# The down products of a group of MLP units placed one up block later, behind the next group's first block, in a two-layer decoder trunk on one core

## Chip, cores and metric

The kernel runs on one core of one Trainium2 chip. The metric is device time in microseconds (us) from the first to the last instruction's end, as the runs report it; lower is better.

## The reference

One inference step of a two-layer decoder trunk, in float32, over 1,024 prompt tokens and 32 new tokens (1,056 columns). Layer 0 is a gated linear recurrence, layer 1 dilated window attention; each ends in an MLP of 4,096 hidden units on a width of 1,024:

```python
def _sqrelu_mlp(x, w_up, w_down):
    return jnp.square(jax.nn.relu(x @ w_up)) @ w_down
...
        x = x + h.astype(x.dtype)
        x = x + _sqrelu_mlp(_rmsnorm(x, mlp_norm[layer]), mlp_w_up[layer], mlp_w_down[layer]).astype(x.dtype)
```

The change lies in the two MLPs alone.

## The kernel before

**Exact pairs.** Each operand of a product is kept as a pair, a rounded high part and the low rest. A product of 128 by 128 weights with a chunk of tokens is three matmuls: high by high, high by low, low by high (L182 to L184 for the up blocks, L772 to L774 for the down products). The tokens lie in three chunks of 384, 384 and 288 columns (c = 0, 1, 2).

**Groups.** `mlp` goes over the 32 blocks of hidden units in eight groups (`NG`) of four. For each group it makes the four up blocks, j = 0 to 3, and after them the down products of the group, which add into the residual `xr`. An up block is 72 matmuls: for each chunk eight steps of K by three. Its results leave PSUM chunk by chunk in `ev_up`: ScalarE takes the relu into `tmp` (L716), VectorE squares it (L717), ScalarE makes the high part (`hbH`, `hH`, L705), VectorE or GpSimd the low part (`hbL`, `hL`, L706).

**Two by two blocks.** The first two chunks are multiplied down by seven products in place of eight, on sums and differences of the blocks. So `ev_up` also makes differences of squares on VectorE (L722, L739) and splits them: at chunk 1 of block 0 and of block 2 one, at chunk 1 of block 1 and of block 3 three. For the last group of a layer there are no differences, and its down products are the plain ones.

**Down products.** For the first seven groups `down` is called four times, for two output blocks at a time. In PE's order one call is: product into bank A (six matmuls of 384 columns), into C (a bank of the pool `g`), into B, a second one into A, the third chunk of the first output (twelve matmuls of 288), into B, into A, the third chunk of the second output, into A. Between two products into the same bank VectorE has added the bank to `xr` (L786; L208 for the third chunk): the second product into A waits for the first `add` of A, the last product into A waits for the third one.

**Weights.** `weight_order` lists the weights in their order of use; `wnext` hands out one and prepares the next (`_prep`). SyncE loads 256 KB twice into `wraw` (two buffers); ScalarE rounds the halves to `whi` and GpSimd makes `wlo` (L128, L129). `whi` and `wlo` have two buffers, so those of a weight are made when PE has finished the last weight but one. A down weight of the first seven groups also needs its own sums and differences `wsum` (VectorE L156 to L158, GpSimd L159), again rounded to `whix` and `wlox` (two buffers). A `wraw` buffer comes free when its `wlo` and `wsum` have been made.

**What sets the order.** The scheduler orders each engine's instructions before the run, by priorities (weights are given a head start of 400 instructions, the relu of 200, the adds of 30); on the chip each engine keeps to its order.

Of the kernel before, what the change touches and what calls it, by code (L numbers as in the profile page):

```python
# [10 lines left out]
F32 = mybir.dt.float32  # L11
F32R = mybir.dt.float32r
# [14 lines left out]
# the chunks of the MLPs: a pair for the products of two by two blocks, and one alone  # L27
# [14 lines left out]
def view(t, off, *dims):  # L42
    """Columns off + sum of steps of a [P, n] tile, by (step, count)."""
    return bass.AP(t.tensor, t.offset + off, [t.ap[0], *([s, n] for s, n in dims)])


class Kern:
# [48 lines left out]
    def weight_order(self):  # L96
# [25 lines left out]
    def _prep(self, i):  # L122
# [54 lines left out]
    def mm3(self, ps, w, x, ks):  # L177
        """ps = sum over (kw, kx) of w[:, kw]^T x[:, kx], both as exact pairs."""
# [14 lines left out]
    def proj_n(self, ws, ops, evacs):  # L193
        """Blocks of 128 outputs over all tokens, the chunks of tokens outside."""
# [15 lines left out]
    def accum(self, items, ops, chunk_outer):  # L210
        """x[m] += w^T ops for the items (m, w, pairs of k)."""
# [7 lines left out]
    def quarter_items(self, tiles, off):  # L219
        """Tiles of two output blocks by four blocks of K each."""  # L220
# [26 lines left out]
    def norm(self, gi, ops, need, gaps=(3, 3, 2), hp=0):  # L247
        """The normalized residual as pairs, chunk by chunk, after the steps of the products that fill them."""
# [36 lines left out]
    def phase_a(self):  # L285
# [44 lines left out]
        def sigmoid(x, mul):  # L330
            """x to sigmoid(x) = exp(min(x, 0) - ln(1 + exp(-|x|))), or to its product with x."""
# [12 lines left out]
        def ev_f(h, b, kt, lf):  # L344
            def ev(c, ps):
# [22 lines left out]
                # reversed chunks: from sums over the later tokens to sums over the earlier ones  # L368
# [40 lines left out]
        # output projection  # L409
# [31 lines left out]
    def gla_levels(self, b, kt, q, levels, A):  # L441
        """A[s, t] for 128 tokens in runs of twice the first level."""
# [20 lines left out]
    def transp(self, dst, src, n, w=P):  # L463
        """dst[:, c, :] = src[:, c*w:(c+1)*w]^T"""
# [6 lines left out]
    def decays(self, b, kt, q):  # L471
        """For the new tokens, k decayed to the end of its run, q decayed from its start, the runs' decays."""
# [30 lines left out]
    def scores(self, i, pair, A):  # L503
        """A[s, t] of level i: a pair of chunks by one product."""
# [13 lines left out]
    def chunk_decays(self, b, kt, q):  # L518
        """k decayed to the end of its chunk, q decayed from the start of its own, the chunks' decays."""
# [13 lines left out]
    def gla(self, h, b, kt, q, vT, og):  # L533
        """A head over the prompt, in steps."""
# [6 lines left out]
        def ahead(n):  # L541
            """The operands of the levels and of the states of both halves, made up to the n-th."""
# [154 lines left out]
    def mlp(self, layer, ops, after=None):  # L697
# [6 lines left out]
        def split(dst, i, x, pool=False):  # L704
            nc.scalar.activation(dst[0][:, i, :], x, AF.Copy)  # L705
            (nc.gpsimd if pool else nc.vector).tensor_tensor(dst[1][:, i, :], x, dst[0][:, i, :].bitcast(F32), op=ALU.subtract)  # L706

        def ev_up(hs, hb, j, tmp, last):
            """Blocks j of the hidden units: rows j % 2 of the two by two blocks, at j // 2 of them."""
            i, e = divmod(j, 2)  # L710

            def ev(c, ps):
# [5 lines left out]
                if c == 2:  # L718
                    return split(hs, 2 * e + i, r, True)
                tmp[e, c] = r  # L720
                # of b11, b12, b21, b22 and their combinations
                sub = lambda x, y: nc.vector.tensor_tensor(x, y, x, op=ALU.subtract)  # L722
                h = hb[i]
                if c == 0:
                    split(h, e, r, True)
                elif last:
                    split(h, 2 + e, r)
                elif e == 0:
                    t = tmp[0, 0]
                    sub(t, r)  # L730
                    split(h, 3, t)
                else:
                    split(h, 2, r)
                    t2, t3, t4 = tmp[0, 0], tmp[0, 1], tmp[1, 0]
                    sub(t3, r)
                    split(h, 5, t3)
                    sub(t2, r)
                    split(h, 4, t2)
                    nc.vector.tensor_tensor(t4, t4, t2, op=ALU.subtract)  # L739
                    split(h, 6, t4)  # L740
            return ev

        two = lambda shape, name, bufs: [hpool.tile(shape, F32R, name=name + x, bufs=bufs) for x in "HL"]
        for g in range(NG):
            hs = two([P, GS, 288], "h", 1)
            hb = [two([P, 7, PW], "hb", 2) for _ in range(2)]
            tmps = [{}, {}]
            evs = [ev_up(hs, hb, j, tmps[j // 2], g == NG - 1) for j in range(GS)]
            for ev in evs:
                self.proj(self.wnext(), ops, ev)  # L750
            if g < NG - 1:
                for p in range(4):
                    self.down(2 * p, self.wnext(), hs, hb)
            else:
                w = [self.wnext() for _ in range(4)]
                if after:
                    self.lanes.append(self.norm(None, after, NEED))
                for c in range(NCH):
                    for m in range(8):
                        at = lambda k: (hs, k) if c == 2 else (hb[k % 2], 2 * c + k // 2)  # L760
                        ps = self.proj_bank(c)
                        self.mmx(ps, [(w[m // 2], 4 * (m % 2) + k, *at(k)) for k in range(4)])
                        self.resid(m, c, ps)
                        self.tick()
# [3 lines left out]
    def mmx(self, ps, items, start=True, stop=True):  # L768
        """ps (+)= sum over (w, kw, x, kx) of w[:, kw]^T x[:, kx]"""
        nc = self.nc  # L770
        for i, ((wh, wl), kw, (xh, xl), kx) in enumerate(items):
            nc.tensor.matmul(ps, wh[:, kw, :], xh[:, kx, :], start=start and i == 0, stop=False, skip_group_check=True)  # L772
            nc.tensor.matmul(ps, wh[:, kw, :], xl[:, kx, :], start=False, stop=False, skip_group_check=True)  # L773
            nc.tensor.matmul(ps, wl[:, kw, :], xh[:, kx, :], start=False, stop=stop and i == len(items) - 1, skip_group_check=True)  # L774
# [662 lines left out]
```

## Time and profile before

| | |
|---|---|
| median of three runs | 3062.18 us (3060.68 to 3073.53) |
| span of the profiled execution | 3067.9 us, inside the spread of the runs; no other time is recorded for it |
| PE busy in that span | 2899.6 us, 95% |
| VectorE, ScalarE, GpSimd busy | 58%, 42%, 44% |
| up blocks of one group (288 matmuls) | 46.48 us |
| down products of one group (264 matmuls), 14 times | 45.46 to 48.28 us |

A busy PE counts the modelled ends of pipelined matmuls, so the starts of matmuls tell more than the busy share. In rows of a timeline, what stands in brackets is the idle time of the engine before the instruction, and what ended it.

### The profile page before, as it was taken

What the parts mean: (1) busy time and instruction counts of PE and PEld (TensorE: products, weight loads), DVE (VectorE), ACT (ScalarE), POOL (GpSimd) and SP (SyncE); (2) the same over time, 40 slices, a digit from 0 to 9 for tenths busy, and PEclk for the clock granted to TensorE, in tenths of its full rate; (3) what the DMA queues carried; (4) which work ended last, traced back from release to release, by engine and by line L of the source; (5) the groups of instructions that cost most, each with busy time, mean ns of one, the idle gap of its engine ahead of it and who ended that gap; (6) DMA issues with size and microseconds to landing.
All of it is one profiled execution on the core that took longest, in us unless ns stands there. A gap on an engine that the chain in (4) does not pass through costs nothing.

```text
span 3067.9 us, 47376 instructions
## 1 busy us (share of the span) xinstructions
PE 2899.6 (95%) x18144; PEld 2776.5 (91%) x18144; DVE 1793.7 (58%) x3467; ACT 1281.9 (42%) x2972; POOL 1337.4 (44%) x1149
## 2 busy tenths in 40 slices
PE   6998999899999999999899999999988999999999
PEld 5888888789999999999899889889888999999999
DVE  8777777876554444543654565664676454544442
ACT  6565556643233222232445545555444222333221
POOL 5444444443444444444463454343225444544442
PEclk9999999999999999999999999999999999999999
DMA  3100210230111111111212233332631111111112
GB/s 112 36 29 29 70 40 30 83 106 21 45 46 42 49 49 42 49 42 62 84 61 67 81 100 112 126 116 68 211 127 42 49 42 49 45 45 42 49 49 85
DMA packets 131956, 201.91 MB, mean 66 GB/s; under 512 B 26321, under 2 KB 65873, under 8 KB 129681
## 3 DMA queue, kind: packets, MB, share of 16 engines
q1 hardware_dynamic: 131728, 198.88, 20.2%
q8 instruction: 143, 2.34, 0.3%
q14 instruction: 85, 0.69, 0.1%
HBM read 164.04 MB, written 34.80 MB: 65 GB/s over the span
## 4 chain that ended last, share of the span: by engine, by line
PE 55%; DVE 13%; POOL 7%; issue 7%; DMA 5%; ACT 3%; SPq 0%; POOLq 0%; DVEq 0%; ACTq 0%
PE pj L182 9%; PE pj L183 9%; PE pj L184 9%; PE pj L772 5%; PE pj L773 4%; PE pj L774 4%; POOL wlo L129 4%; PE g L774 3%; DMA wraw<-w_dn 3%; PE g L773 3%; PE g L772 2%; PE g L1110 2%; PE g L1082 1%; DVE tmp L717 1%; POOL wlox L129 1%
## 5 line engine op out<-in xcount | busy, mean ns | idle before, releaser
L182 PE MATMUL pj<-opH,whi 128*128 128x352 f32 (+2 forms) x3408 | 1138.3, 334 | 9.6 <-ACT opH L229 4.7
L183 PE MATMUL pj<-opL,whi 128*128 128x352 f32 (+2 forms) x3408 | 1111.8, 326 | 3.8 <-POOL opL L230 3.1
L184 PE MATMUL pj<-opH,wlo 128*128 128x352 f32 (+2 forms) x3408 | 1109.0, 326 | 3.0 <-POOL wlo L129 2.7
L129 POOL TENSOR_TENSOR wlo<-wraw,whi 128x512 fp32r<-128x512 f32 x404 | 546.0, 1370 | 938.9 <-ACT whi L128 896.1
L182 PEld LDWEIGHTS pj<-opH,whi 128*128 128x128 f32 x3408 | 647.7, 190 | 30.3 <-issue 16.0
L183 PEld LDWEIGHTS pj<-opL,whi 128*128 128x128 f32 x3408 | 648.4, 190 | 16.0 <-POOL opL L230 6.2
L184 PEld LDWEIGHTS pj<-opH,wlo 128*128 128x128 f32 x3408 | 647.3, 190 | 6.9 <-POOL wlo L129 4.2
L128 ACT ACTIVATE whi<-wraw 128x512 fp32r<-128x512 f32 x404 | 232.7, 622 | 558.7 <-PE g L773 452.2
L717 DVE TENSOR_TENSOR tmp<-tmp 128x384 f32<-128x384 f32 (+1 forms) x192 | 161.7, 843 | 342.4 <-ACT tmp L716 342.4
L786 DVE TENSOR_TENSOR xr<-xr,pj 128x384 f32<-128x384 f32 x336 | 184.8, 553 | 132.3 <-PE pj L774 132.2
L705 ACT ACTIVATE hbH<-tmp 128x384 fp32r<-128x384 f32 x212 | 109.7, 525 | 245.6 <-DVE tmp L717 150.4
L772 PE MATMUL pj<-hbH,whix 128*128 128x384 f32 x512 | 177.9, 347 | 34.4 <-DVE xr L786 26.0
L773 PE MATMUL pj<-hbL,whix 128*128 128x384 f32 x512 | 175.5, 343 | 5.7 <-DVE hbL L706 5.7
L774 PE MATMUL pj<-hbH,wlox 128*128 128x384 f32 x512 | 174.2, 340 | 0.0
L493 POOL TENSOR_TENSOR lv<-b 128x512 f32<-128x512 f32 x112 | 125.0, 1127 | 104.0 <-PE g L590 59.6
L716 ACT ACTIVATE tmp<-pj 128x384 f32<-128x384 f32 (+1 forms) x192 | 86.9, 453 | 190.5 <-PE pj L184 189.8
L129 POOL TENSOR_TENSOR wlox<-wsum,whix 128x512 fp32r<-128x512 f32 x112 | 151.0, 1370 | 0.0
L772 PEld LDWEIGHTS pj<-hbH,whix 128*128 128x128 f32 x512 | 97.7, 191 | 43.8 <-DVE xr L786 30.5
L774 PE MATMUL g<-hH,wlo 128*128 128x288 f32 x448 | 137.1, 306 | 0.0
L773 PE MATMUL g<-hL,whi 128*128 128x288 f32 x448 | 136.4, 305 | 0.0
L772 PE MATMUL g<-hH,whi 128*128 128x288 f32 x448 | 135.4, 302 | 0.0
L1084 DVE CUSTOM_DVE_ANT_0 pr<-g,band,rq 128x128 f32<-128x128 f32 (+1 forms) x192 | 68.0, 405 | 79.3 <-PE g L1082 75.6
(343 smaller groups left out, 5371.9 us busy)
## 6 DMA issues: line engine op xcount, KB each, us to landing
wraw<-w_up SPq DMA_DIRECT2D x128, 256.0 KB, 2.7
wraw<-w_dn SPq DMA_DIRECT2D x128, 256.0 KB, 2.6
wraw<-w_in SPq DMA_DIRECT2D x64, 256.0 KB, 2.7
wraw<-w_q SPq DMA_DIRECT2D x48, 256.0 KB, 2.8
ub<-us SPq DMA_DIRECT2D x32, 256.0 KB, 2.2
cc<-ck SPq DMA_DIRECT2D x8, 1024.0 KB, 4.9
cc<-cv SPq DMA_DIRECT2D x8, 1024.0 KB, 5.4
wraw<-w_kv SPq DMA_DIRECT2D x24, 256.0 KB, 2.9
```

Of the source, the lines that this page charges most:

```text
L128: nc.scalar.activation(hi[:, j:j + 4, :], raw, AF.Copy)
L129: nc.gpsimd.tensor_tensor(lo[:, j:j + 4, :], raw, hi[:, j:j + 4, :].bitcast(F32), op=ALU.subtract)
L182: nc.tensor.matmul(ps, wh[:, kw, :], xh[:, kx, :], start=(i == 0), stop=False)
L183: nc.tensor.matmul(ps, wh[:, kw, :], xl[:, kx, :], start=False, stop=False)
L184: nc.tensor.matmul(ps, wl[:, kw, :], xh[:, kx, :], start=False, stop=(i == len(ks) - 1))
L493: nc.gpsimd.tensor_tensor(r(lv), r(b), r(b)[:, :, h - 1:h].to_broadcast([P, 256 // h, 2 * h]), op=ALU.subtract)
L705: nc.scalar.activation(dst[0][:, i, :], x, AF.Copy)
L717: nc.vector.tensor_tensor(r, r, r, op=ALU.mult)
L772: nc.tensor.matmul(ps, wh[:, kw, :], xh[:, kx, :], start=start and i == 0, stop=False, skip_group_check=True)
L773: nc.tensor.matmul(ps, wh[:, kw, :], xl[:, kx, :], start=False, stop=False, skip_group_check=True)
L774: nc.tensor.matmul(ps, wl[:, kw, :], xh[:, kx, :], start=False, stop=stop and i == len(items) - 1, skip_group_check=True)
L786: self.nc.vector.tensor_tensor(x(i, c), x(i, c), ps, op=ALU.add)
```

## The change

The down products of group g - 1 now stand behind block 0 of group g, and blocks 1 to 3 of group g follow them. The order of the weights is changed alike. Block 0's values must live while the group before is still being multiplied, so they get tiles of their own with two buffers (`h0` for the third chunk, `hp` for the two values of the first two); the rest (`h`, `hq`, `hb`) have one buffer each and are allocated at block 1. `split` and `mmx` now take a value's own pair of columns and no index. The last group's down products stand where they stood, behind its four blocks. The rest of the diff takes out comments and makes a scratch area for DMAs smaller; the order of instructions outside the MLPs is the same in both.

```diff
         def mlp(layer):
-            for g in range(ng):
-                q.extend((a["w_up"][layer, g * GS + j], None, False) for j in range(GS))
-                q.extend((a["w_dn"][layer, g, i], None, g == ng - 1 and i in (1, 2)) if g == ng - 1
-                         else (a["w_dn"][layer, g, i], None, False, True) for i in range(GS))
+            up = lambda g, js: q.extend((a["w_up"][layer, g * GS + j], None, False) for j in js)
+            up(0, range(GS))
+            for g in range(ng - 1):
+                up(g + 1, (0,))
+                q.extend((a["w_dn"][layer, g, i], None, False, True) for i in range(GS))
+                up(g + 1, range(1, GS))
+            q.extend((a["w_dn"][layer, ng - 1, i], None, i in (1, 2)) for i in range(GS))
...
-            evs = [ev_up(hs, hb, j, tmps[j // 2], g == NG - 1) for j in range(GS)]
-            for ev in evs:
-                self.proj(self.wnext(), ops, ev)
-            if g < NG - 1:
-                for p in range(4):
-                    self.down(2 * p, self.wnext(), hs, hb)
...
+            early = (0, 2) if last else (0, 3)
...
+            a, b = two([P, 1, 288], "h0", 2), two([P, 2, PW], "hp", 2)
...
+            def rest():
+                a, b, c = two([P, 3, 288], "h", 1), two([P, 5, PW], "hq", 1), two([P, 7, PW], "hb", 1)
...
+        made = {}
+        for g in range(NG + 1):
+            if g < NG:
+                hs, hb, rest = hidden(g)
+                tmps = [{}, {}]
+                made[g] = hs, hb, rest, [ev_up(hs, hb, j, tmps[j // 2], g == NG - 1) for j in range(GS)]
+                ups(g, (0,))
+            if g:
+                hs, hb = made.pop(g - 1)[:2]
+                if g < NG:
+                    for p in range(4):
+                        self.down(2 * p, self.wnext(), hs, hb)
+            if g < NG:
+                ups(g, range(1, GS))
```

On VectorE, this stands before where block 3 of a group ends and its first down call begins. `tmp` with 384 or 288 columns is a square or a difference, `hbL` a low part, `xr` an add, `wsum` (here of the third down weight) a sum of weights:

```order
L717 TENSOR_TENSOR tmp<-tmp 128x384
L722 TENSOR_TENSOR tmp<-tmp 128x384 x2
L706 TENSOR_TENSOR hbL<-tmp,hbH 128x384 x3
L739 TENSOR_TENSOR tmp<-tmp 128x384
L786 TENSOR_TENSOR xr<-xr,pj 128x384
L717 TENSOR_TENSOR tmp<-tmp 128x288
L706 TENSOR_TENSOR hbL<-tmp,hbH 128x384
L786 TENSOR_TENSOR xr<-xr,g 128x384
L786 TENSOR_TENSOR xr<-xr,pj 128x384 x2
L156 TENSOR_TENSOR wsum<-wraw 128x256
L158 TENSOR_TENSOR wsum<-wraw 128x256
L157 TENSOR_TENSOR wsum<-wsum,wraw 128x256
```

The first add of A stood behind the whole chain of block 3. In the changed kernel, the same place, from block 3's last low part (`hbL`) over block 0 of the next group (`hpL`) into the first down call; the `wsum` here is that of the second down weight:

```order
L710 TENSOR_TENSOR hbL<-tmp,hbH 128x384
L159 TENSOR_TENSOR wsum<-wraw 128x256
L721 TENSOR_TENSOR tmp<-tmp 128x384
L160 TENSOR_TENSOR wsum<-wsum,wraw 128x256
L161 TENSOR_TENSOR wsum<-wraw 128x256
L721 TENSOR_TENSOR tmp<-tmp 128x384
L726 TENSOR_TENSOR tmp<-tmp 128x384
L710 TENSOR_TENSOR hpL<-tmp,hpH 128x384
L819 TENSOR_TENSOR xr<-xr,pj 128x384
L721 TENSOR_TENSOR tmp<-tmp 128x288
L819 TENSOR_TENSOR xr<-xr,g 128x384
L819 TENSOR_TENSOR xr<-xr,pj 128x384 x2
```

The first add of A now stands behind block 0's chunk 1, and that behind the `wsum` of the second weight. What follows on VectorE there is the `wsum` of the third weight, then the adds of the rest of the first call (third chunk, the second of B, the third of A):

```order
L159 TENSOR_TENSOR wsum<-wraw 128x256
L161 TENSOR_TENSOR wsum<-wraw 128x256
L160 TENSOR_TENSOR wsum<-wsum,wraw 128x256
L211 TENSOR_TENSOR xr<-xr,g 128x288
L819 TENSOR_TENSOR xr<-xr,pj 128x384 x2
```

These five rows stand in the same order in both kernels. On ScalarE, before, from block 3's chunk 1 on (`hbH x3`), the two `whi` are those of the second and then of the third down weight:

```order
L705 ACTIVATE hbH<-tmp 128x384 x3
L128 ACTIVATE whi<-wraw 128x512 x2
L716 ACTIVATE tmp<-pj 128x288
L705 ACTIVATE hbH<-tmp 128x384
L705 ACTIVATE hH<-tmp 128x288
L128 ACTIVATE whi<-wraw 128x512 x2
L128 ACTIVATE whix<-wsum 128x512 x2
```

In the changed kernel, from the same `hbH x3`; the first `whi` is now that of the first down weight, the second that of the second, behind block 0's chunk 1:

```order
L709 ACTIVATE hbH<-tmp 128x384 x3
L131 ACTIVATE whi<-wraw 128x512 x2
L720 ACTIVATE tmp<-pj 128x288
L709 ACTIVATE hbH<-tmp 128x384
L709 ACTIVATE hH<-tmp 128x288
L720 ACTIVATE tmp<-pj 128x384
L709 ACTIVATE hpH<-tmp 128x384
L131 ACTIVATE whix<-wsum 128x512 x2
L720 ACTIVATE tmp<-pj 128x384
L709 ACTIVATE hpH<-tmp 128x384
L131 ACTIVATE whi<-wraw 128x512 x2
```

Each step of the preparation has moved one block of the program on.

## Rows read from the trace of the kernel before

**Rows 1.** The page: busy us, share of the span and instructions by engine.

```profile
PE 2899.6 (95%) x18144; PEld 2776.5 (91%) x18144; DVE 1793.7 (58%) x3467; ACT 1281.9 (42%) x2972; POOL 1337.4 (44%) x1149
```

**Rows 2.** Windows, down products: length; busy PE, PEld, DVE, ACT, POOL; clock third from last.

```profile
887.26:934.24 46.98, 44.31 (x266) 43.30 (x265) 27.57 (x50) 10.29 (x20) 20.18 (x18) 0.96 0.15 46
980.73:1026.42 45.69, 42.68 (x266) 41.79 (x265) 27.64 (x50) 10.30 (x20) 20.55 (x18) 1.00 0.16 47
1072.91:1118.37 45.46, 42.70 (x266) 41.81 (x265) 27.41 (x50) 10.30 (x20) 20.30 (x18) 1.00 0.14 47
...
2926.38:2971.87 45.49, 42.70 (x267) 41.80 (x265) 27.43 (x50) 10.30 (x20) 20.33 (x18) 1.00 0.15 47
sum 656.32, PE 616.21 PEld 603.36 DVE 387.55 ACT 144.19 POOL 285.40; mean PE 44.01 PEld 43.10 DVE 27.68 ACT 10.30 POOL 20.39
```

**Rows 3.** Windows: the four up blocks ahead of the first of these.

```profile
840.78:887.26 46.48, 46.48 (x289) 46.48 (x289) 18.24 (x29) 16.80 (x35) 22.42 (x20) 1.00 0.15 46
```

**Rows 4.** Timeline of PE: first down call (three rows), third, start of the fourth.

```profile
890.43 0.44 PE L772 MATMUL pj<-hbH,whix 128*128 128x384 f32 x1 [0.40 <-ACT hbH L705]
891.28 0.44 PE L773 MATMUL pj<-hbL,whix 128*128 128x384 f32 x1 [0.41 <-DVE hbL L706]
893.75 0.69 PE L772 MATMUL pj<-hbH,whix 128*128 128x384 f32 x1 [1.86 <-DVE xr L786]
...
913.31 0.33 PE L772 MATMUL pj<-hbH,whi 128*128 128x384 f32 x1
...
916.43 0.34 PE L772 MATMUL pj<-hbH,whix 128*128 128x384 f32 x1
...
922.73 0.34 PE L772 MATMUL pj<-hbH,whix 128*128 128x384 f32 x1
...
923.78 0.33 PE L772 MATMUL pj<-hbH,whi 128*128 128x384 f32 x1
```

**Rows 5.** Timeline of DVE, from block 2 (starts 864.02) to the down call (887.26).

```profile
870.60 0.42 DVE L156 TENSOR_TENSOR wsum<-wraw 128x256 f32<-128x256 f32 x1 [2.52 <-DMA wraw<-w_dn]
...
875.52 1.46 DVE L722 TENSOR_TENSOR tmp<-tmp 128x384 f32<-128x384 f32 x1
877.57 0.56 DVE L706 TENSOR_TENSOR hbL<-tmp,hbH 128x384 fp32r<-128x384 f32 x1 [0.59 <-ACT hbH L705]
...
883.44 0.43 DVE L156 TENSOR_TENSOR wsum<-wraw 128x256 f32<-128x256 f32 x1 [3.70 <-DMA wraw<-w_dn]
...
893.16 0.54 DVE L786 TENSOR_TENSOR xr<-xr,pj 128x384 f32<-128x384 f32 x1
...
897.32 0.43 DVE L156 TENSOR_TENSOR wsum<-wraw 128x256 f32<-128x256 f32 x1 [0.69 <-DMA wraw<-w_dn]
...
898.34 0.45 DVE L208 TENSOR_TENSOR xr<-xr,g 128x288 f32<-128x288 f32 x1
```

**Rows 6.** Timeline of ACT: the high parts of down weights at the ends of blocks 2, 3.

```profile
877.44 1.14 ACT L128 ACTIVATE whi<-wraw 128x512 fp32r<-128x512 f32 x2
...
890.75 1.14 ACT L128 ACTIVATE whi<-wraw 128x512 fp32r<-128x512 f32 x2
```

**Rows 7.** Timeline of POOL: low parts of weights at the ends of blocks 1, 2, 3.

```profile
864.85 2.81 POOL L129 TENSOR_TENSOR wlo<-wraw,whi 128x512 fp32r<-128x512 f32 x2 [5.31 <-ACT whi L128]
...
878.14 2.75 POOL L129 TENSOR_TENSOR wlo<-wraw,whi 128x512 fp32r<-128x512 f32 x2 [1.58 <-ACT whi L128]
...
891.44 2.92 POOL L129 TENSOR_TENSOR wlo<-wraw,whi 128x512 fp32r<-128x512 f32 x2 [2.04 <-ACT whi L128]
```

**Rows 8.** Windows behind three waits, columns as in rows 2.

```profile
893.76:897.17 3.41, 3.41 (x12) 3.41 (x13) 2.87 (x5) 0.48 (x2) 1.41 (x2) 0.50 0.55 154
1170.24:1177.07 6.83, 5.23 (x19) 5.23 (x20) 5.60 (x11) 0.99 (x3) 3.25 (x4) 0.50 0.29 78
1489.38:1496.34 6.96, 6.96 (x50) 6.75 (x50) 5.60 (x8) 2.93 (x6) 4.17 (x4) 1.00 0.39 115
```

**Rows 9.** Timeline of PE: the wait ahead of the last of these windows.

```profile
1489.38 0.86 PE L270 MATMUL g<-sqacc,onesD 128*128 128x352 f32 x2 [2.20 <-DVE sqacc L264]
```

More of the change, by code (lines that the diff above doesn't have):

```diff
@@ L718, in ev @@
                 if c == 2:
-                    return split(hs, 2 * e + i, r, True)
+                    return split(hs[2 * e + i], r, True)
                 tmp[e, c] = r
@@ L724, in ev @@
                 if c == 0:
-                    split(h, e, r, True)
+                    split(h[e], r, True)
                 elif last:
-                    split(h, 2 + e, r)
+                    split(h[2 + e], r)
                 elif e == 0:
@@ L730, in ev @@
                     sub(t, r)
-                    split(h, 3, t)
+                    split(h[3], t)
                 else:
-                    split(h, 2, r)
+                    split(h[2], r)
                     t2, t3, t4 = tmp[0, 0], tmp[0, 1], tmp[1, 0]
                     sub(t3, r)
-                    split(h, 5, t3)
+                    split(h[5], t3)
                     sub(t2, r)
-                    split(h, 4, t2)
+                    split(h[4], t2)
                     nc.vector.tensor_tensor(t4, t4, t2, op=ALU.subtract)
-                    split(h, 6, t4)
+                    split(h[6], t4)
@@ L741, in ev_up, with hidden @@
             return ev
[L743 to L747, printed above, removed]
-            evs = [ev_up(hs, hb, j, tmps[j // 2], g == NG - 1) for j in range(GS)]
-            for ev in evs:
-                self.proj(self.wnext(), ops, ev)
-            if g < NG - 1:
-                for p in range(4):
-                    self.down(2 * p, self.wnext(), hs, hb)
[L754 to L764, printed above, removed]
+        def hidden(g):
+            last = g == NG - 1
+            early = (0, 2) if last else (0, 3)
+            two = lambda shape, name, bufs: [hpool.tile(shape, F32R, name=name + x, bufs=bufs) for x in "HL"]
+            cut = lambda t, k: tuple(x[:, k] for x in t)
+            hs, hb = {}, ({}, {})
+            a, b = two([P, 1, 288], "h0", 2), two([P, 2, PW], "hp", 2)
+            hs[0] = cut(a, 0)
+            for n, k in enumerate(early):
+                hb[0][k] = cut(b, n)
+            def rest():
+                a, b, c = two([P, 3, 288], "h", 1), two([P, 5, PW], "hq", 1), two([P, 7, PW], "hb", 1)
+                hs.update((k, cut(a, k - 1)) for k in range(1, 4))
+                hb[0].update((k, cut(b, n)) for n, k in enumerate(k for k in range(7) if k not in early))
+                hb[1].update((k, cut(c, k)) for k in range(7))
+            return hs, hb, rest
@@ new lines, in ups @@
+        def ups(g, js):
+            hs, hb, rest, evs = made[g]
+            for j in js:
+                if j == 1:
+                    rest()
+                self.proj(self.wnext(), ops, evs[j])
+        made = {}
[12 more added lines that the diff above has]
+                ups(g, range(1, GS))
@@ L765, in mlp @@
+        w = [self.wnext() for _ in range(4)]
+        if after:
+            self.lanes.append(self.norm(None, after, NEED))
+        for c in range(NCH):
+            for m in range(8):
+                at = lambda k: hs[k] if c == 2 else hb[k % 2][2 * c + k // 2]
+                ps = self.proj_bank(c)
+                self.mmx(ps, [(w[m // 2], 4 * (m % 2) + k, at(k)) for k in range(4)])
+                self.resid(m, c, ps)
+                self.tick()
         ctx.close()
@@ L770, in mmx @@
         nc = self.nc
[L771 to L774, printed above, removed]
+        for i, ((wh, wl), kw, (xh, xl)) in enumerate(items):
+            nc.tensor.matmul(ps, wh[:, kw, :], xh, start=start and i == 0, stop=False, skip_group_check=True)
+            nc.tensor.matmul(ps, wh[:, kw, :], xl, start=False, stop=False, skip_group_check=True)
+            nc.tensor.matmul(ps, wl[:, kw, :], xh, start=False, stop=stop and i == len(items) - 1, skip_group_check=True)
     def down(self, m, ws, hs, hb):
@@ L781, in prod @@
         def prod(ps, w, kw, b, start=False, stop=False):
-            self.mmx(ps, [(w, kw + i, hb[i], b) for i in range(2)], start, stop)
+            self.mmx(ps, [(w, kw + i, hb[i][b]) for i in range(2)], start, stop)
         def add(i, c, ps):
@@ L789, in alone @@
             ps = self.bank()[:, :288]
-            self.mmx(ps, [(w, 4 * i + k, hs, k) for k in range(4)])
+            self.mmx(ps, [(w, 4 * i + k, hs[k]) for k in range(4)])
             self.resid(m + i, 2, ps)
```

9 lines of the change are left out of this document (5 added, 4 removed).

## Prediction

> **What bounds the kernel now.** I read the page first: PE is busy for 95% of the span, so it sets the time, and only its gaps can be won [rows 1]. The windows by stage show where the change can act. Four up blocks of a group take 46.48 us at full clock with PE never idle [rows 3], so a block takes 11.62. The down products of the first seven groups of a layer, 14 stretches, take 656.32 us together [rows 2]. What they would take without a wait shows in the timeline of PE: the third call of such a stretch runs from 913.31 to 923.78, 10.47 us, and four of them make 41.88 [rows 4]. So 656.32 less 14 × 41.88 = 586.3 leaves 70.0 us lost, 5.0 for each stretch.
>
> The first call shows the loss: PE waits 0.40 and 0.41 for the last values of block 3, then 1.86 for VectorE's add of bank A [rows 4]; that add runs only at 893.16, behind the chain of squares, differences and low parts of block 3 [rows 5], although block 3 ended at 887.26. Behind it the granted clock is 0.50 for 3.41 us, that is 1.2 in place of 2.4 GHz, and half of that stretch is lost too [rows 8]. Three stretches keep the full clock: 45.69, 45.46 and 45.49 [rows 2], 3.67 over 41.88 on average. 14 × 3.67 = 51.3 us are then waits and restarts, and the other 18.7 the clock, which falls in 11 of the 14.
>
> **The change, part by part.** Nothing is added or removed: the same matmuls, evacuations, loads. Block 0 of the next group, 11.62 us of PE work, comes between block 3 and the first down call. Block 3's chain ended 5.9 us after its block (893.16) and now has 11.62: the waits for its values (0.40, 0.41) go, and the add no longer stands behind that chain. Moved too are block 0's own evacuation, ahead of the first call, and the weights, for each is prepared when PE has done with the last but one. The `whi` of the first down weight, so far made at the end of block 2 (877.44 [rows 6]), is made at the end of block 3, that of the second at the end of the added block. In VectorE's order the second weight's `wsum`, which waits for its load, stands ahead of all squares of the added block, and these ahead of the first add; so PE's wait may come back by that way. I follow it with the durations of the same steps in blocks 2 and 3 of before.
>
> Step 1, block 3. Block 2 before it now prepares no down weight, as block 1 so far: after such a block `wlo` is done at 864.85 + 2.81 = 867.66 [rows 7], and the next `wsum` runs at 870.60 [rows 5], 6.58 after the block's end at 864.02. So the first weight's `wsum` comes 6.58 into block 3. From `wsum` to the next `whi` took 7.31 in block 3 (883.44 [rows 5] to 890.75 [rows 6]), three high parts between them: `whi` at 13.89, which is 2.27 into the added block. From there to the end of `wlo` took 3.61 (890.75 to 891.44 + 2.92 = 894.36 [rows 7]): 5.88.
>
> Step 2, the load. `wlo` frees the `wraw` buffer, and the next weight's `wsum` ran 2.55 (880.89 to 883.44) and 2.96 (894.36 to 897.32) after it [rows 5, 7]. These are my bounds; I take 2.75 between them. The second weight's `wsum` then runs 8.63 into the added block.
>
> Step 3, the first wait. From `wsum` to the end of chunk 1's low part took 7.53 in block 2 (870.60 to 877.57 + 0.56 [rows 5]), and the added block has block 2's work: one difference. 8.63 + 7.53 = 16.16, and the add with 0.54 ends at 16.70, 5.08 after the added block. PE wants it after three products, 3.12 into the call (913.31 to 916.43 [rows 4]). It waits **1.96 us**.
>
> Step 4, the second wait. From `wsum` to `whi` took 6.84 in block 2 (870.60 to 877.44 [rows 5, 6]), so the second weight's `whi` stands at 15.47, 3.85 after the added block. `wlo` ends 3.45 later, as 877.44 to 880.89, at 7.30, and the third weight's `wsum` runs at 10.05. Ahead of the last product into A stand, on VectorE, the three `wsum` (1.02, 897.32 to 898.34), the add of a third chunk (0.45) and two adds (0.54 each): 12.60. PE without any wait wants A at 9.42 (913.31 to 922.73 [rows 4]). So the call ends **3.2 us** late in all, the first wait being part of it. With the loads at their bounds, each entering twice, it is 2.8 or 3.6.
>
> What hides the rest: the second and third call find their weights as now, since all that follows `whi` of the third weight hangs on PE's end of the first call, as before. Block 1 writes tiles that the last down call has read; its first value is ready only after its chunk 0, 24 matmuls on, so this waits for nothing, and without that cover it would cost the 1 us of a relu and a square.
>
> In the last stretch of a layer the added block belongs to the last group, which has no difference: 1.46 less [rows 5] on both waits. So 12 × 3.2 + 2 × 1.74 = 41.9 us of lateness against the 70.0 of now.
>
> The clock. It fell behind waits of 0.40, 0.41 and 1.86 within 4 us; behind a single wait of 2.20 [rows 9] it stayed at 1.00 [rows 8]. The new waits are 1.96 and, 6 us on, 1.2, so I expect few falls and allow one in four. Behind the first wait a fall takes 1.71 but eats the second wait, 0.5 in the end; behind the second it takes 1.71. At a mean of 1.1, 14 × 0.25 × 1.1 = 3.9 us.
>
> Sum: 41.9 + 3.9 = 45.8 against 70.0, a gain of 24.2 us. The profiled span of 3067.9 lies 5.7 above the median of 3062.18, inside the spread of the runs; taken from the span it gives 3043.7, taken from the median, by which I forecast, **3038**.
>
> **Rivals.** *The clock falls as often as now (R1).* The waits last 3.2 as before but the 18.7 us stay: 60.6, a gain of 9.4, 3053. For it: 11 of 14 fall now. Against it: the waits are shorter and apart.
>
> The Trainium skill, "TensorE: Matmul & The Clock Gate", section "A second HAM failure mode: psum-queue depth-cycling", says that short idles between groups of matmuls that go round the PSUM banks can make the clock swing between its levels. By that rule R1 or the last rival would hold; the 2.20 us wait without a fall speaks against it, the 11 falls for it.
>
> *Only the first wait is left (R2).* If the third weight's load lands under 7 us after the added block, not at 10, the adds are there in time: 12 × 1.96 + 2 × 0.5 = 24.5, a gain of 45.5, 3017. For it: the chain has four steps each of which I took from another block.
>
> *All is hidden (R3).* If the add comes 2 us earlier as well, the whole 70.0 are won: 2992. It needs the second weight's `wsum` before 6.7 us into the added block, where 8.4 is the earliest by the bounds.
>
> *Slower (R4).* The clock falls behind the second wait and stays low for 6.83 us, as it did at 1170.24 [rows 8], in every stretch: 41.9 + 14 × 3.42 = 89.8, 19.8 more than now, 3082. It turns slower where a stretch loses over 5.0 us, so with more than 1.8 of clock each. For it stands that two idles follow each other where one group of idles stood; against it that only two of the 14 now have the long fall.
>
> **How the numbers follow.** The forecast has a chance of 0.50, R1 0.20, R2 0.14, R3 0.08, R4 0.08. Alone, the forecast reaches from 3029 (2.8 a stretch, no fall) to 3047 (3.6, and a fall in half of them). The range runs to R2's and R1's sides, 3012 to 3057, and leaves out R3, R4 and the ends. 0.5% is 15 us, about what measurement can tell here: faster by that are the forecast but for 0.05 of it, R2 and R3, 0.67; the same R1 and that rest, 0.25; slower R4, 0.08.
>
> **What would show it.** In the profile after, PE's first down call has no wait for a high or low part of block 3; a wait of about 2 us ahead of the second product into A, ended by VectorE's add; about 1.2 ahead of the last product into A, ended by the add behind the third weight's `wsum`; that `wsum` about 10 us after the call's start; stretches of down products of about 45 us. The up blocks should stay at 11.62. I am wrong if the `wsum` of the second weight comes before 7 us of the added block (then R2 or R3), if clocks of 0.96 or less stand in most stretches (R1), or if a wait appears at the first evacuation of block 1, which would be a cause that I have put at nothing.

## The result and the profile after

The changed kernel takes 3042.76 us (median of 4 runs, 3040.48 to 3045.13), against 3064.42 us of the kernel before in the same comparison: a ratio of 0.9931 (95% interval 0.9907 to 0.9954), so 0.7% less. The forecast was 3038, with a range of 3012 to 3057.

The page of the profiled execution after, busy time by engine (compare [rows 1]):

```profile
PE 2875.0 (94%) x18144; PEld 2757.8 (91%) x18144; DVE 1796.0 (59%) x3467; ACT 1282.9 (42%) x2972; POOL 1338.3 (44%) x1149
```

Its span is 3043.4 us, 24.5 shorter than the 3067.9 of before. The windows of the 14 down stretches answer to [rows 2]; columns: window, length, busy PE, granted clock, DMA share, GB/s.

```profile
801.38:846.69 45.31, 42.42 (x266) 1.00 0.15 47
893.18:940.74 47.56, 44.18 (x267) 0.96 0.14 45
...
1355.53:1399.96 44.43, 42.42 (x267) 1.00 0.15 48
...
sum 637.39, PE 600.91; mean PE 42.92
```

The 14 stretches together have become 18.9 us shorter (656.32 to 637.39), and 51.1 us are still left above the 586.3 of no wait. The clock falls in 4 of them in place of 11. The up blocks stay at 46.49 (846.69 to 893.18), without idle time of PE, against 46.48 in [rows 3].

Where PE waits in the first down call of the stretch at 893.18, after (timeline of PE; the bracket is the idle time and what ended it; compare [rows 4]):

```profile
898.08 0.44 PE L805 MATMUL pj<-hqH,whix 128*128 128x384 f32 x1 [1.61 <-DVE xr L819]
...
906.48 0.54 PE L805 MATMUL pj<-hqH,whix 128*128 128x384 f32 x1 [1.77 <-DVE xr L819]
```

The waits for values of block 3 are gone. Two are left, 4.9 and 13.3 us after the call's start, both ended by VectorE's add, as forecast. The timeline of VectorE shows what stands ahead of these adds (compare [rows 5]):

```profile
890.04 0.42 DVE L159 TENSOR_TENSOR wsum<-wraw 128x256 f32<-128x256 f32 x1 [1.76 <-DMA wraw<-w_dn]
...
893.29 1.57 DVE L721 TENSOR_TENSOR tmp<-tmp 128x384 f32<-128x384 f32 x1 [1.68 <-ACT tmp L720]
894.96 1.46 DVE L726 TENSOR_TENSOR tmp<-tmp 128x384 f32<-128x384 f32 x1
...
897.48 0.55 DVE L819 TENSOR_TENSOR xr<-xr,pj 128x384 f32<-128x384 f32 x1
...
904.03 0.43 DVE L159 TENSOR_TENSOR wsum<-wraw 128x256 f32<-128x256 f32 x1 [3.47 <-DMA wraw<-w_dn]
...
905.41 1.01 DVE L819 TENSOR_TENSOR xr<-xr,pj 128x384 f32<-128x384 f32 x2
```

VectorE stands still twice, 1.76 and 3.47 us, in front of the sums of a down weight (`wsum`) until a load has landed, with the square, the difference and the adds behind it. A third stop, 1.68 us at 893.29, is for ScalarE's relu of the added block's second chunk. PE had begun the chunk after that one at 889.98, but on ScalarE the relu stands behind the high parts of the same sums:

```profile
892.24 0.63 ACT L131 ACTIVATE whix<-wsum 128x512 fp32r<-128x512 f32 x1 [0.22 <-POOL wsum L162]
892.78 0.47 ACT L720 ACTIVATE tmp<-pj 128x384 f32<-128x384 f32 x1
```

So the sums that wait for a load hold up the added block twice, in VectorE's order and in ScalarE's.

### The profile page after: what moved, and what is told of

The parts are those of the page before. It is cut to its first block, busy times and chain, and to the rows that moved or that the text cites. A ratio compares the mean times of both kernels' runs of the same rounds, so it can differ in the third digit from the quotient of the medians.

```text
span 3043.4 us, 47407 instructions
## 1 busy us (share of the span) xinstructions
PE 2875.0 (94%) x18144; PEld 2757.8 (91%) x18144; DVE 1796.0 (59%) x3467; ACT 1282.9 (42%) x2972; POOL 1338.3 (44%) x1149
## 4 chain that ended last, share of the span: by engine, by line
PE 56%; DVE 10%; POOL 8%; issue 7%; DMA 5%; ACT 3%; POOLq 0%; SPq 0%; DVEq 0%; ACTq 0%
PE pj L185 10%; PE pj L186 10%; PE pj L187 10%; POOL wlo L132 4%; PE pj L805 4%; PE pj L806 4%; PE pj L807 4%; DMA wraw<-w_dn 3%; PE g L806 2%; PE g L805 2%; PE g L807 2%; POOL wlox L132 2%; PE g L1143 2%; PE g L1115 1%; PE g L1130 1%
## 5 line engine op out<-in xcount | busy, mean ns | idle before, releaser
L721 DVE TENSOR_TENSOR tmp<-tmp 128x384 f32<-128x384 f32 (+1 forms) x192 | 169.5, 883 | 311.2 <-ACT tmp L720 311.2
L162 POOL TENSOR_TENSOR wsum<-wraw,wsum 128x256 f32<-128x256 f32 x56 | 43.7, 781 | 168.0 <-DVE wsum L160 153.8
L1120 ACT ACTIVATE pr<-pr,nm 128x128 f32<-128x128 f32 (+1 forms) x192 | 84.1, 440 | 68.0 <-DVE nm L1118 67.8
L148 POOL TENSOR_TENSOR wraw<-wraw,gains 128x512 f32<-128x512 f32 x72 | 91.4, 1275 | 40.0 <-DMA wraw<-w_q 33.3
L211 DVE TENSOR_TENSOR xr<-xr,pj 128x384 f32<-128x384 f32 (+1 forms) x132 | 67.2, 516 | 69.7 <-PE pj L187 37.5
L709 ACT ACTIVATE hbH<-tmp 128x384 fp32r<-128x384 f32 x106 | 54.9, 526 | 121.2 <-DVE tmp L721 72.8
L967 POOL TENSOR_TENSOR q<-q,cos 32x512 f32<-32x512 f32 x48 | 89.8, 1877 | 30.2 <-DVE rsw L966 28.9
L159 DVE TENSOR_TENSOR wsum<-wraw 128x256 f32<-128x256 f32 x56 | 23.8, 425 | 131.5 <-DMA wraw<-w_dn 131.3
L806 PE MATMUL g<-hL,whi 128*128 128x288 f32 x336 | 100.5, 299 | 0.0
```

What stands on the lines that cost most here:

```text
L148: nc.gpsimd.tensor_tensor(raw, raw, self.gains[:, gi, j:j + 4][:, :, None].to_broadcast([P, 4, P]), op=ALU.mult)
L721: nc.vector.tensor_tensor(r, r, r, op=ALU.mult)
L806: nc.tensor.matmul(ps, wh[:, kw, :], xl, start=False, stop=False, skip_group_check=True)
```

## The experiments

My account at this point: the waits that are left come from VectorE's order, in which the second and third weight's sums stand ahead of work that PE waits for, and wait for a load. The rivals: the added block's own evacuation makes the add late, or the tiles of their own make the gain and not the new place. Ratios are against the kernel before on the same chip.

**Only the tiles.** The tiles of after with the loops of before, and the order of the weights with them; core of the diff to the changed kernel:

```diff
-                ups(g, (0,))
+            ups(g, range(GS))
...
-                hs, hb = made.pop(g - 1)[:2]
...
                         self.down(2 * p, self.wnext(), hs, hb)
-            if g < NG:
-                ups(g, range(1, GS))
```

> Tiles as in the changed kernel (first block's values and the other values apart), but the down products stay where they were before the change, directly behind block 3; the program order of every engine is that of before. My account (the gain comes from the place of the down products): the time of before, 3064 within 6 us, down stretches of about 47 us. Rival (the other tiles, or where they lie, make the gain): about 3043.

Measured: 0.9995 (0.9981 to 1.001), 3071.11 us against 3070.71. The 14 stretches of the profiled execution sum to 664.44; the clock fell in 13 of them, before in 11. By the medians the tiles cost and give nothing, and the gain comes from the place.

**Sums late.** The making of the sums becomes a function, called at once for a group's first weight and for the others in the down call before theirs; two copies of one column, which read the residual after the second add, hold the place. The rounding of the sums to `whix` and `wlox` is part of the function, so ScalarE's and GpSimd's work on them moves too:

```diff
+            def sums(behind=None):
                 t, u = (self.wx.tile([P, 4, P], F32, name="wsum") for _ in range(2))
+                if behind is not None:
+                    nc.vector.tensor_copy(t[:, 0, :1], behind)
+                    nc.vector.tensor_copy(u[:, 0, :1], behind)
                 tt(t[:, :2], a21, a22, op=ALU.add)
...
+            if self.wq[i - 1][3:]:
+                self.late = sums
...
         add(0, 0, C)
+        if self.late:
+            with self.tc.high_priority(offset=20):
+                self.late(x(0, 0)[:, :1])
+            self.late = None
         add(1, 1, B)
```

> The changed kernel, but the sums of the second, third and fourth down weight of a group stand later in VectorE's order: behind the second add of the down call before theirs (two one-column copies hold them there), no longer ahead of the squares of the added block and of the last adds. Loads, buffers and all work are as in the changed kernel. My account (VectorE waits in front of these sums for the load, at 8.6 us into the added block and at 10 to 11 us of the call, and the adds stand behind): both waits of TensorE go, a down stretch takes 41.9 to 42.5 us, the clock has no reason to fall, 3043 less 14 x 3.6 is about 2995 (2988 to 3005). The margin is thin at one place: the low part of the second weight's sums is ready about 12 us after the call's start and wanted at 12.6. Rival A (the added block's own evacuation, a square, a difference and a low part, is what makes the add late): both waits stay, 3043. Rival B (the waits only move on to the second call, which now lacks its sums): 3035 to 3045 with a wait at the second call's third product.

Measured: 0.9767 (0.9748 to 0.9787), 2998.59 us. Windows of its down stretches:

```profile
888.30:930.38 42.08, 42.08 (x267) 1.00 0.17 51
...
sum 587.36, PE 587.36; mean PE 41.95
```

PE is busy in all of 587.36 us, and the clock stays at 1.00 in all 14. Its VectorE, in the first call of the stretch at 888.30:

```profile
889.54 0.56 DVE L829 TENSOR_TENSOR xr<-xr,pj 128x384 f32<-128x384 f32 x1 [1.04 <-PE pj L817]
...
891.37 0.75 DVE L164 TENSOR_TENSOR wsum<-wraw 128x256 f32<-128x256 f32 x1
```

Now the add waits for PE (1.04) and not PE for the add; the sums run 3.1 us into the call and find their load there. The added block's own evacuation is still in front of the add, so that rival has fallen, and so has the one that sends the wait on to the second call: no stretch has a wait.

**Only the second weight's sums late**, then **only the third's and fourth's**. The condition is all that differs from the run above:

```diff
-            if self.wq[i - 1][3:]:
+            if self.wq[i - 1][3:] and not self.wq[i - 2][3:]:
```

```diff
-            if self.wq[i - 1][3:]:
+            if self.wq[i - 2][3:]:
```

> As the run with late sums, but only the second weight's sums are late; the third weight's stay ahead of the last adds of the first call. My account (the first wait is part of the lateness that the third weight's load sets; the sum of the two is 3.2 us whatever the first is): the first wait goes, the wait ahead of the last product grows from 1.2-1.7 to 2.5-3.5 us and ends again 12 to 13 us after the call's start; the stretch stays at about 45 us, 3043 within 7 us, and a clock that falls more often would be the only cost. Rival (the two waits are independent and add up): 14 x 1.8 = 25 us less, 3018.

> As the run with late sums, but the second weight's sums stay ahead of the added block's squares; the third's and fourth's are late. My account: the first wait stays at 1.6 to 1.9 us and ends 5 us after the call's start, the second goes; the stretch is 43.7 us, 14 x 1.4 = 20 us less than 3043, and some us more where the clock no longer falls: 3022 (3016 to 3028). Rival (the second wait comes from the adds themselves or from the clock behind the first wait, not from the third weight's load): 3043.

Measured: 0.9822 (0.9802 to 0.9843), 3016.45 us, and 0.9853 (0.9834 to 0.9872), 3024.64 us. The second of the two came as I expected: the first wait stays at 1.64 to 1.89 us outside the last stretch of a layer, and the other is gone. In the first I was wrong by 27 us: the wait ahead of the last product did not grow to 2.5-3.5 us; one wait of 0.54 to 1.72 us is left. The rival's time, 3018, came out. Why is in its trace. ScalarE, GpSimd and VectorE in the stretch that starts at 896.28:

```profile
896.35 1.16 ACT L132 ACTIVATE whi<-wraw 128x512 fp32r<-128x512 f32 x2 [0.31 <-PE pj L196]
```

```profile
897.06 2.76 POOL L133 TENSOR_TENSOR wlo<-wraw,whi 128x512 fp32r<-128x512 f32 x2 [2.66 <-ACT whi L132]
...
901.19 0.79 POOL L167 TENSOR_TENSOR wsum<-wraw,wsum 128x256 f32<-128x256 f32 x1 [0.43 <-DVE wsum L165]
```

```profile
906.14 0.42 DVE L164 TENSOR_TENSOR wsum<-wraw 128x256 f32<-128x256 f32 x1 [2.29 <-DMA wraw<-w_dn]
906.48 0.55 DVE L829 TENSOR_TENSOR xr<-xr,pj 128x384 f32<-128x384 f32 x1
```

The second weight's `whi` comes 0.07 us after the call's start; in the changed kernel it came 3.70 after it (896.88, below), because there it stands on ScalarE behind the added block's last high part, which the second weight's sums had held up. So the low parts end 3.54 after the start and not 7.14. What then keeps the raw tile is the fourth sum on GpSimd, to 901.98, and the third weight's sums run 9.86 after the start in place of 10.85. The add that PE waits for ends 10.75 after the start (906.48 + 0.55) and not 13.24, 2.49 earlier. Of this, 0.99 is the earlier load; the other 1.50 is order: here that add stands right behind the first of these sums, while in the changed kernel all three sums, the third chunk's add and another add stand ahead of it. My expectation had taken the time of the third load and the order of the last adds as the same with the second weight's sums late, and neither was; step 4 of the prediction ties the load to those sums, by way of `whi`. The rival's two waits that add up are not shown either, for the wait that is left changed too.

**The old place, sums late.** The kernel before, with the edit of the run with late sums and nothing else. So the sums and their rounding move, and the down products stay behind block 3.

> The kernel before (down products directly behind block 3), with the one edit of the run with late sums: the second, third and fourth weight's sums stand behind the second add of the call before. It asks whether the late sums alone would have done it. My account: no. In the run with late sums block 3's own chain of squares, differences and low parts still ran until about 6 us after block 3's end with nothing in front of it, because the operations take 1.0 to 1.6 us each there; in the old place the first add stands behind it, some 0.6 us earlier than the 5.9 us of before. A gain of 0 to 2 us for each of 14 stretches: 3064 less 14 = 3050 (3036 to 3064). Rival (the sums in front of the adds are the whole cause in both kernels, the place of the down products does not matter): 2995 to 3010.

Measured: 0.9762 (0.9737 to 0.9787), 2994.2 us. My account is wrong here and the rival right: the late sums alone win all of it, without the move. The windows, columns as above:

```profile
878.30:920.16 41.86, 41.86 (x266) 1.00 0.17 51
...
sum 586.16, PE 586.16; mean PE 41.87
```

No stretch has a wait. Block 3's chain on VectorE before (block 3 ends at 887.26, the add ends at 893.70 [rows 5]), the rows of ScalarE ahead of it, and GpSimd beside it:

```profile
886.67 1.58 DVE L717 TENSOR_TENSOR tmp<-tmp 128x384 f32<-128x384 f32 x1 [1.67 <-ACT tmp L716]
888.28 2.00 DVE L722 TENSOR_TENSOR tmp<-tmp 128x384 f32<-128x384 f32 x2
...
891.61 1.62 DVE L739 TENSOR_TENSOR tmp<-tmp 128x384 f32<-128x384 f32 x1
```

```profile
884.37 0.53 ACT L705 ACTIVATE hbH<-tmp 128x384 fp32r<-128x384 f32 x1 [3.76 <-DVE tmp L717]
...
885.63 0.63 ACT L128 ACTIVATE whix<-wsum 128x512 fp32r<-128x512 f32 x1 [0.22 <-POOL wsum L159]
886.17 0.47 ACT L716 ACTIVATE tmp<-pj 128x384 f32<-128x384 f32 x1
```

```profile
886.53 2.87 POOL L129 TENSOR_TENSOR wlox<-wsum,whix 128x512 fp32r<-128x512 f32 x2
```

And the same chain in the old place with late sums (block 3 ends at 878.30):

```profile
875.88 0.56 DVE L727 TENSOR_TENSOR tmp<-tmp 128x384 f32<-128x384 f32 x1 [3.47 <-ACT tmp L726]
876.47 1.02 DVE L732 TENSOR_TENSOR tmp<-tmp 128x384 f32<-128x384 f32 x2
877.42 1.49 DVE L716 TENSOR_TENSOR hbL<-tmp,hbH 128x384 fp32r<-128x384 f32 x3
878.82 0.55 DVE L749 TENSOR_TENSOR tmp<-tmp 128x384 f32<-128x384 f32 x1
879.54 0.56 DVE L796 TENSOR_TENSOR xr<-xr,pj 128x384 f32<-128x384 f32 x1 [0.17 <-PE pj L784]
```

```profile
875.36 0.49 ACT L726 ACTIVATE tmp<-pj 128x384 f32<-128x384 f32 x1 [2.39 <-PE pj L194]
```

```profile
879.08 2.91 POOL L130 TENSOR_TENSOR wlo<-wraw,whi 128x512 fp32r<-128x512 f32 x2 [5.01 <-ACT whi L129]
```

The add ends 1.80 us after block 3 and not 6.44. Of these 4.64 us, 1.83 are an earlier start (the second chunk's square 2.42 ahead of the block's end and not 0.59), since nothing of block 3 stands behind a load any more. Before, the way went from VectorE to ScalarE and back: the first chunk's square stood behind the sum that waited for the load (883.44 [rows 5]), its high part (884.37) waited for the square, the high parts of the sums followed, and only then came the second chunk's relu (886.17). Now that relu (875.36) waits for PE alone. The other 2.81 are shorter operations (7.03 from the square to the add's end against 4.22). Before, the square and the two differences ran beside the low parts of the sums (886.53 to 889.40) and the last difference beside the next weight's low parts (891.44 [rows 7]); now GpSimd idles 5.01 us, up to 879.08, and the square takes 0.56 us, the two differences 1.02, the last one 0.55.

**A load more under way.** The changed kernel, with raw tiles of their own for every second down weight and four tiles for sums:

```diff
-                raw = (self.wx if x is True and self.rawx else self.wp).tile(...)
+                raw = (self.wx if early or x is True and self.rawx else self.wp).tile(...)
-                t, u = (self.wx.tile([P, 4, P], F32, name="wsum") for _ in range(2))
+                t, u = (self.wx.tile([P, 4, P], F32, name="wsum", bufs=4) for _ in range(2))
```

> The changed kernel, but the raw tiles of every second down weight come from two buffers of their own, and there are four buffers for the sums in place of two, so that one load more can be under way. My account: no gain, 3043 within 8 us. Every engine's order moves up by one weight with it: the second weight's sums now stand in block 3 and the third's where the second's stood, ahead of the added block's squares, and their load still waits for the low parts of the first weight, 5.9 us into the added block; the fourth's stand ahead of the last adds and wait for those of the second weight. So both waits end where they ended, 5.0 and 13 us after the call's start. Rival (the load is too late only because there are too few raw tiles; a tile more hides it): both waits go, 2995 to 3010.

Measured: 1.0022 (1.0006 to 1.0038), 3074.43 us: no gain, as expected, but it also lost all that the change had won, which I had not expected. So the rival has fallen as it was stated: with these two more raw tiles the waits did not go. What I had left out is ScalarE's order; its timeline in the stretch whose added block begins at 884.66 and whose call starts at 896.28:

```profile
886.57 0.63 ACT L138 ACTIVATE whix<-wsum 128x512 fp32r<-128x512 f32 x1 [1.21 <-POOL wsum L170]
887.10 0.47 ACT L728 ACTIVATE tmp<-pj 128x384 f32<-128x384 f32 x1
...
890.70 1.14 ACT L138 ACTIVATE whi<-wraw 128x512 fp32r<-128x512 f32 x2
```

The relu of block 3's second chunk now stands behind the high parts of the sums of two weights, and runs 2.44 us after the block's end. The first weight's `whi` comes 6.04 us into the added block and not 2.27, and the third weight's sums, ahead of the added block's squares, run 1.04 us after the call's start where I had them 3.0 ahead of it (897.32). PE waits 3.44 us once, ahead of the second product into A.

**The sums on GpSimd.** The changed kernel, one line:

```diff
-                tt = nc.vector.tensor_tensor
+                tt = nc.gpsimd.tensor_tensor
```

> The changed kernel, but the three sums that VectorE makes of a down weight are made on GpSimd, in its order where the fourth already stands; loads and buffers as in the changed kernel. VectorE then waits for no load. My account (what matters is who stands in line behind the load): both waits go, 2990 to 3010. GpSimd makes 3 x 0.8 us more per weight and waits for the loads itself, so the low parts of the first weights come 2 us later, 9 us after the call's start, still ahead of their need at 10.5; the third load starts later, which now stops nobody. Rival A (GpSimd's 2.4 us are on the path: weights late at the second call): 3020 to 3045 with a wait at the start of the second or third call. Rival B (GpSimd's additional work slows VectorE's squares beside it so much that the first add is late all the same): 3020 to 3043 with the first wait kept.

Measured: 0.9957 (0.9936 to 0.9978), 3055.83 us; not the 2990 to 3010 of my account. VectorE waits for no load any more, but PE still waits, once, ahead of the second product into A: 3.15 to 3.69 us, and 1.07 and 1.27 in the last stretches of a layer. So rival A's wait in a later call is not there. ScalarE, then PE, in the stretch that starts at 896.22:

```profile
896.13 0.63 ACT L131 ACTIVATE whix<-wsum 128x512 fp32r<-128x512 f32 x1 [3.62 <-POOL wsum L160]
...
897.08 0.62 ACT L131 ACTIVATE whix<-wsum 128x512 fp32r<-128x512 f32 x1
897.60 0.47 ACT L720 ACTIVATE tmp<-pj 128x384 f32<-128x384 f32 x1
```

```profile
902.84 0.44 PE L805 MATMUL pj<-hqH,whix 128*128 128x384 f32 x1 [3.33 <-DVE xr L819]
```

ScalarE's line is left: the sums' high parts stand ahead of the added block's second relu, as they do in the changed kernel (892.78, 0.40 us ahead of that block's end). GpSimd has the sums ready later, so here the relu runs 1.38 us after the block's end. GpSimd's own line adds to it: the difference of that block waits another 0.91 us for one of the block's low parts, which stands on GpSimd behind a low part of the sums, and then takes 1.60 us beside the next of these (899.57 on VectorE), so rival B has a share. To tell all this from a GpSimd that is simply too slow, the same sums on GpSimd, but late:

> The run with late sums (added block ahead of the down products, second to fourth weight's sums behind the second add of the call before), with the three sums made on GpSimd in place of VectorE. It asks why the sums on GpSimd won nothing when they stayed early: there ScalarE's high parts of the sums stood ahead of its relu of the added block's second chunk and waited for GpSimd (896.13 and 897.08, relu at 897.60, call start 896.22). My account (a line through ScalarE in place of the one through VectorE; GpSimd's own 0.74 us per sum is no bound): with the sums late it is gone, no wait, down stretches of 41.9 to 42.2, 2990 to 3005, ratio to before 0.977. Rival (GpSimd is too slow for these sums, or slows VectorE beside it): 3030 to 3056, with a wait at the first add or at a later call's third product.

Measured: 0.9769 (0.9743 to 0.9795), 2994.98 us. Its stretches:

```profile
sum 587.36, PE 587.36; mean PE 41.95
```

So GpSimd is fast enough, and the place in line is what costs, on whichever engine. How much of the 3.3 us was ScalarE's line and how much GpSimd's, no run tells apart.

## Why the prediction was right, and where it was not

**Steps 1 to 3 held.** For the stretch at 893.18 (its added block begins at 881.56) the weights' parts after are these, of ScalarE and of GpSimd:

```profile
883.83 1.14 ACT L131 ACTIVATE whi<-wraw 128x512 fp32r<-128x512 f32 x2
...
896.88 1.13 ACT L131 ACTIVATE whi<-wraw 128x512 fp32r<-128x512 f32 x2
```

```profile
884.52 2.97 POOL L132 TENSOR_TENSOR wlo<-wraw,whi 128x512 fp32r<-128x512 f32 x2 [2.04 <-ACT whi L131]
...
897.57 2.75 POOL L132 TENSOR_TENSOR wlo<-wraw,whi 128x512 fp32r<-128x512 f32 x2 [1.57 <-ACT whi L131]
```

| | forecast | measured |
|---|---|---|
| first weight's `whi`, into the added block | 2.27 | 2.27 |
| its `wlo` done, into the added block | 5.88 | 5.93 |
| second weight's sums, into the added block | 8.63 | 8.48 |
| first add done, after the call's start | 5.08 | 4.85 |
| PE's first wait | 1.96 | 1.61 |
| second weight's `whi`, after the call's start | 3.85 | 3.70 |
| its `wlo` done, after the call's start | 7.30 | 7.14 |
| third weight's sums, after the call's start | 10.05 | 10.85 |
| adds done, after the call's start | 12.60 | 13.24 |

One reading was short and did no harm. Block 3's chain before did not end at 893.16, where the add starts, but with a low part at 895.16, 7.90 us after its block; 11.62 cover that as well.

**Step 4, a size.** In this stretch the third weight's sums came 3.71 us after `wlo` and not 2.75: its two loads took 2.7 to 3.0 us to land in most stretches, and up to 3.7, where the second weight's took 2.4 to 2.5 in most, which I had taken for both. The eight full-clock stretches that are not the last of a layer took 45.39 on average, 3.51 us late against the forecast 3.2.

**The last stretch of a layer, a size.** The added block there has no difference, for which I took off 1.46 from both waits. The stretches are 44.43 and 44.35, 2.5 us late in place of 1.74; the first wait was 1.04 and 0.95, not 0.5.

**The clock: the sum held, its reason did not.** Four falls cost 3.9 us (185.48 in the four stretches less 4 x 45.39), as forecast. But I had reasoned from a single wait of 2.20 us without a fall [rows 8, 9] that single waits bring few. In the changed kernel three of the four falls came behind the first wait, of 1.79 to 1.94 us, with no other wait of the stretch ahead of it; a window of one:

```profile
1084.17:1087.60 3.43, 3.41 (x12) 0.50 0.33 86
```

In these three the second wait was gone or down to 0.30 us, and the fall cost 0.6 us on average, near the 0.5 that I had put for it; the one behind a second wait cost 2.2. With the second wait taken away the clock fell in four stretches all the same, behind a lone wait of 1.72 to 1.89 us; here in the run with only the third's and fourth's sums late (PE, then windows):

```profile
810.54 0.44 PE L815 MATMUL pj<-hqH,whix 128*128 128x384 f32 x1 [1.89 <-DVE xr L829]
```

```profile
811.77:815.77 4.00, 4.00 (x19) 0.57 0.45 131
```

Behind a lone wait of 3.15 to 3.69 us, with the sums on GpSimd, it fell in 5 of 12 stretches; behind 0.54 to 1.72 us, with the second weight's sums late, in none of 14; with raw tiles of their own, behind 3.44 to 4.22 us, in 10 of 12. The Trainium skill, "TensorE: Matmul & The Clock Gate", section "A second HAM failure mode: psum-queue depth-cycling", has the clock swing with short idles between groups of matmuls; the traces agree that such idles can bring it down, in 11 of 14 stretches before and in 4 of 14 after. So R1, as many falls as before, did not come.

**The sum.** Forecast was 45.8 us of lateness, measured are 51.1, so the stretches gave 18.9 and not 24.2. The clock's part held, and waits and restarts were 47.2 in place of 41.9, by the two sizes above. The span's other 5.6 us lie outside the stretches: 3.9 ahead of the first MLP's down products (the added block at 801.38 - 11.62 = 789.76 after, that stretch at 793.68 before), 1.5 between the MLPs, and 0.1 behind them. Kernels that are alike up to there come to this point between 788.33 and 794.25 (the runs with late sums, and with the second's late), so the 3.9 are within scatter; the 1.5 I did not follow. That the spans lie 24.5 us apart, as the forecast of 24.2 has it, is therefore luck in part; the medians lie 21.7 apart.

**What I took for the cause.** The forecast of the changed kernel was right, its account of the kernel before stopped one step short. It put the loss of before on block 3's chain, behind which the add stood, so that a block of cover seemed to be what it needed. The old place with late sums shows what the chain stood behind: the second weight's sums, which [rows 5] show at 883.44 and which waited 3.70 us for a load, then ScalarE's high parts of these sums, ahead of the relu, and GpSimd's low parts of weights and sums beside it. R3 (all hidden, 2992) was therefore to be had, but I had tied it to an earlier load; what it takes is a later place in line. The move itself only put 11.62 us between the late chain and its reader, and led the second weight's sums, which wait as before, in front of the same add.

Both places of the down products take the same time with late sums, 0.9767 and 0.9762; in the old place the kernel needs neither the new loops nor the tiles of their own, so with late sums the change is not needed.

## What to carry to other kernels

Where an add is late behind a chain, follow the chain up to its first wait before giving it cover: here one operation that waits for a load stood ahead of work that was ready, and putting it behind that work took the down stretches from 656 to 586 us, where the cover took them to 637. The operations on other engines that wait for it count as well: with the sums made on GpSimd at their early place 0.4% was won, with the same sums late 2.3%. So look, on every engine in the chain, for what waits for a transfer and stands ahead of ready work, and ask how late its reader allows it to be. Two more raw tiles did not help here, for they moved the whole line up by one.

## What the runs showed of the hardware

**VectorE beside GpSimd.** Its square of 128x384, with both operands in SBUF, took 0.56 us where GpSimd was idle (875.88 in the old place with late sums) and 1.58 beside GpSimd's low parts (886.67 before); the chain of seven operations and the add was 2.81 us longer there. GpSimd loses less: two low parts took 2.75 to 2.97 us there and 2.54 where VectorE had only adds from PSUM (at 908.26 in the run with only the second weight's sums late). The Trainium skill, "SBUF — State Buffer", section "SBUF: two separate sides", says that the two engines share a pair of ports as an exclusive lock: for an operation of VectorE with two inputs in SBUF against one of GpSimd that reads SBUF, whichever starts first has the pair for the whole instruction, and the other blocks. The traces fit in that an operation of VectorE grew by about 1 us and not in proportion to its size (a sum of 128x256 took 0.42 us alone, at 904.37 after, and 1.50 beside low parts, at 883.18 in the run with raw tiles of their own), which is less than one of GpSimd's operations (about 1.4), and in that an add with one input in PSUM kept its 0.54 beside them (893.16 before). Who holds the pair when, no trace shows.

**The clock behind a lone wait.** With only the third's and fourth's sums late, a lone wait of PE brought the clock down in some stretches and not in others, at the same length (1.72 to 1.89 us with a fall, 1.64 to 1.89 without). What decides between them no run here shows.
